# Bias tables in steps inside the first feed-forward part, and a separate operand place at the value stage

## The chip, the cores and the metric

The kernel runs on one core of one Trainium2 chip. Times are device microseconds of one execution; the time before is the median of three runs, 1962.17 us (1961.43 to 1962.37).

The core has five engines that run their own instruction queues in order: TensorE (PE in the profile; PEld is its weight load), VectorE (DVE), ScalarE (ACT), GpSimd (POOL) and SyncE (SP). DMAs are issued from SP, POOL and, at the start, ACT.

## The reference

One encoder layer over `x` of 1024 rows by 1024 columns, float32:

- `x += 1/2 * rmsnorm(swiglu(rmsnorm(x)))`, a feed-forward part with 2816 hidden columns: `(silu(h @ w_gate) * (h @ w_up)) @ w_down`
- `x += rmsnorm(w_out of the attention)`: one projection of `rmsnorm(x)` to q, k and v; 8 heads of neighbourhood attention on a 16 by 64 grid with a learned relative bias (`na_rel_bias`, 8 x 15 x 31), and 8 heads of a mixture of three dilated windows with a bucketed relative bias (`t5_rel_bias`, 8 x 32), each group normalised
- a second feed-forward part like the first

The two relative biases depend on nothing that the layer computes. They are turned into tables in device memory before the attention reads them.

## The kernel before

**Arithmetic.** Every product is float32 made of three matmuls: each operand is split into a high part (a cast on ACT) and a low part (a subtraction on DVE), and `mm3` (lines 249 to 253) adds high*high, high*low and low*high. The large products also use a seven-product scheme on 2 by 2 blocks (`PASSES`, line 31): sums of blocks are made first (S1 to S4 of the left operand, T1 to T4 of the right), and the seven results are combined on DVE.

**Stages in order.** First feed-forward part: gate and up products of 22 hidden blocks (`PairGemm`, about 97 to 500 us of the span for its main loop), then the down products (`Passes`, 500 to 682). Then the values of the attention begin (`Passes`, passes 0 and 1 of 7, 682 to 711), then the early part of the q/k products (`PairGemm.ahead`, 8 pairs, to about 760), then the values' passes 2 to 6 (to about 824), then the q/k products' main loop (`PairGemm.run`), the attention itself, the output projection and the second feed-forward part.

**`PairGemm`** (line 323). `ahead` makes the two products of the first block column for the "early" pairs, with only the left weight blocks: `fetch_left` loads them from SP, `split_left` splits them (ACT, then DVE) into tiles of the pool `wr`, and after a split the load two pairs ahead goes out. `run` makes the rest: per early pair five products of twelve matmuls each, per other pair seven. Weights of a pair are loaded two pairs ahead (`prepare(b)`, whose last step fetches `b + 2`), then turned into T1 to T4 on DVE (lines 432 to 434) and split (lines 344 and 345). A product of pair b that needs the whole pair before (`last`, line 502) is made inside the next pair's turn. At the end of each pair `c.tick()` runs one entry of the list `c.todo`, which is how side work is given turns.

**`Passes`** (line 571). `fetch` loads two raw operand blocks from SP into the pool `pw`, and splits them into the pool `pr` (lines 602 and 603). `run` makes a pass by groups of up to four operands: for each of four row tiles all matmuls of the group go into that tile's PSUM bank, then the result is taken and `c.tick()` is called. For the feed-forward part, whose two operands both come from memory (`own`), pass 0 begins with a group of two and a group of two; for the values each pass is one group of four. `vearly` (line 1360) copies each result of the values' first two passes on ACT into one of two tiles and stores it from POOL.

**Order.** PE's order is the order of the program (`ordered()`, line 1123). The orders of ACT, DVE, POOL and SP are laid out when the kernel is built, by a planner that starts from the program's order and from its own estimates of every instruction's time, except in the first microseconds, where ACT and DVE are in the program's order too. `c.behind(f, engine)` ties what `f` issues on an engine behind the last instruction that the program has given to it so far; `queued` does that for SP and POOL.

**Places.** On-chip tiles come from pools that are opened and closed in stages. A new pool reuses the space of closed ones, and a tile in it is free when the older tiles in that space have been used for the last time. At the start of the values the pools `pr` (three buffers), `pw` (two) and `vt` (two) lie in space of the feed-forward part; when pass 1 ends they close, and `wr` (three buffers of a high and a low tile) opens in the same space for the early q/k pairs.

**The bias tables.** `build_bias` (line 741) is called between the values' passes 3 and 4. It issues, all DMAs from POOL: a small load; twice a pair of loads, one matmul of the one-hot matrix (line 755), an addition on DVE (756), a store of the small table (757) and a write of 8 x 128 rows of 511 numbers (760); a memset and a write of 1536 KB of the mask value (762, 763); eight gathers of short rows into `stk` (765); and sixteen copies from `stk` into the table `nb` (768). Nothing ties the loads of `rel` to the place of the call, and the planner has put those eight DMAs into the first 40 us.

Of the kernel before, what the change touches and what calls it, by code (L numbers as in the profile page):

```python
# [23 lines left out]
NEG = -1e30  # L24
# [298 lines left out]
class PairGemm:  # L323
# [4 lines left out]
    def __init__(self, c, op, srcs, early, sink):  # L328
        self.c, self.op, self.srcs, self.early, self.sink = c, op, srcs, early, sink
        self.n, self.raw, self.w, self.kept = len(srcs), {}, {}, {}  # L330
# [42 lines left out]
    def split_left(self, b):  # L373
        if b < self.early:
            self.w[b] = self.split(self.raw.pop(b), "g")
            self.fetch_left(b + 2)
# [194 lines left out]
class Passes:  # L571
# [4 lines left out]
    def __init__(self, c, n, left, right, take, last=None):  # L576
        self.c, self.left, self.right, self.take = c, left, right, take
        self.own = not isinstance(left, Operand)
        groups = [list(range(i, min(i + 4, n))) for i in range(0, n, 4)]
        self.groups = [groups] * 6 + [last or groups]  # L580
        if self.own:
            self.groups[0] = [groups[0][:2], groups[0][2:]] + groups[1:]
        self.todo = deque((p, g[j:j + 2]) for p in range(7) for g in self.groups[p] for j in range(0, len(g), 2))
        self.ready = deque()

    def fetch(self, w=None, raws=()):
# [4 lines left out]
        if w is None:  # L591
            w = c.pr.tile([P, 1 + self.own, 2, 2, T], F32R, tag="w", name="pw")
            w = [w[:, side] for side in range(1 + self.own)]
        for side in range(1 + self.own):
            raw = raws.popleft() if raws else c.pw.tile([P, 2, T], F32, tag="raw", name="praw")
            if side < self.own:
                nc.sync.dma_start(raw[:, :m], self.left[a][ids[0]:ids[0] + m].rearrange("i p x -> p i x"))
            else:
                for j, i in enumerate(ids):
                    nc.sync.dma_start(raw[:, j], self.right(i)[b])  # L600
            hi, lo = [w[side][:, h, :m] for h in range(2)]
            nc.scalar.copy(hi, raw[:, :m])  # L602
            nc.vector.tensor_sub(lo, raw[:, :m], hi.bitcast(F32))  # L603
        for j, i in enumerate(ids):
            lhs = [w[0][:, h, j, :] for h in range(2)] if self.own else [h[:, i, :] for h in self.left.x[a]]
            self.ready.append((lhs, [w[-1][:, h, j, :] for h in range(2)]))
# [134 lines left out]
def build_bias(c, rel, t5, onehot, lncount):  # L741
# [4 lines left out]
    t5t = c.bp.tile([32, 8], F32, tag="b0", name="t5t")  # L746
    nc.gpsimd.dma_start(t5t, t5.rearrange("h b -> b h"))
    for i in range(2):
        oh = c.bp.tile([P, T], F32, tag="oh", name="oh")
        cols = slice(511 * i, 511 * i + 511)  # L750
        nc.gpsimd.dma_start(oh[:32, :511], onehot[:, cols])
        lc = c.bp.tile([P, T], F32, tag="lc", name="lc")
        nc.gpsimd.dma_start(lc[:8, :511], lncount[:, cols].broadcast_to([8, 511]))
        ps = c.pst.tile([P, 4, P], F32, tag="tr", name="tabp").rearrange("p a b -> p (a b)")
        nc.tensor.matmul(ps[:8, :511], t5t, oh[:32, :511], start=True, stop=True)
# [5 lines left out]
    neg = c.bp.tile([P, T], F32, tag="oh", name="neg")  # L761
    nc.gpsimd.memset(neg[:, :384], NEG)
    nc.gpsimd.dma_start(c.nb.rearrange("h p r e -> p h (r e)"), neg[:, :384].unsqueeze(1).broadcast_to([P, 8, 384]))
    for cc in range(8):
        nc.gpsimd.dma_start(stk[cc], rel[:, :, 7 - cc:31 - cc])
    for r in range(16):
        r0 = min(max(r - 4, 0), 8)
        nc.gpsimd.dma_start(c.nb[:, r * 8:r * 8 + 8, r0:r0 + 8, :].rearrange("h c r e -> c h (r e)"),
                            stk[:, :, r0 - r + 7:r0 - r + 15, :].rearrange("c h r e -> c h (r e)"))
# [339 lines left out]
def layer(tc, a, out):  # L1109
    nc = tc.nc  # L1110
    c = Ctx(tc)
    with ExitStack() as ctx:
# [58 lines left out]
        def one_a_turn(steps, n, first):  # L1171
            plan(n, {first + i: [f] for i, f in enumerate(steps)})
# [11 lines left out]
        def early_pools(stack, n=3):  # L1184
            c.wr, c.sp = pool("wr", 3, stack), pool("sp", n, stack)
# [7 lines left out]
        def ffn(which, op, prep, pg, get, turns, sums, more, post, pre, src, dst, begin=None):  # L1193
# [24 lines left out]
            one_a_turn(sums, NF, NF - 3 - len(sums))  # L1218
            prep2, ps = sub(), []

            def final():
# [9 lines left out]
                ps[0].fetch([w0[:, i] for i in range(2)], raws[:2])  # L1231
                ps[0].fetch([w.rearrange("p (h j) x -> p h j x", h=2) for w in w1], raws[2:])
# [62 lines left out]
        with ExitStack() as order:  # L1295
# [12 lines left out]
            def begin(pg):  # L1308
# [25 lines left out]
                for b in range(2):  # L1334
                    pg.mm(acc[b], pg.w[b], 0, A11, cols=slice(256, 512))
                    s1.append(pg.save(b, acc[b]))
                    if b:
# [12 lines left out]
                                    a["ffn1_post_g"], a["mix_pre_g"], x0, x1, begin)  # L1350
# [5 lines left out]
            c.pr, c.pw, c.vt = pool("pr", 3, e), pool("pw", 2, e), pool("vt", 2, e)  # L1356
# [23 lines left out]
            c.bp = pool("bp", 2, e)  # L1380
# [9 lines left out]
            build_bias(c, a["na_rel_bias"], a["t5_rel_bias"], a["onehot"], a["lncount"])  # L1390
# [211 lines left out]
```

## Time and profile before

| | |
|---|---|
| Median of three runs | 1962.17 us (1961.43 to 1962.37) |
| Profiled execution | 1956.22 us, of which the span from the first to the last instruction is 1954.4 us |
| Mean granted clock of TensorE | 0.986 |
| PE busy | 1867.5 us (96% of the span) |
| DVE busy | 1328.8 us (68%) |
| ACT busy | 807.7 us (41%) |
| POOL busy | 323.8 us (17%) |
| Moved by DMA | 398.63 MB, 204 GB/s on average |

How to read it: an engine's timeline row gives the start in microseconds, the length, the engine, the line of the kernel, the operation, the tile written and those read, and in brackets how long the engine stood idle before it and what ended that. Where several instructions are merged, the row has their count. A matmul's shown length overlaps the next one's. L603 is line 603; a helper's line (344, 345, 602, 603) is shared by many callers, so the tile names tell which work it is: `pw` and `praw` are operands of `Passes`, `graw`, `wraw`, `traw`, `whi` and `wlo` weights of `PairGemm`, `accp` and `mmp` PSUM banks, `vt` and `vs` the early values, `ha` and `hb` the values as they are combined, `gab`, `nb`, `stk`, `tab` and `neg` parts of the bias tables, `g`, `sg`, `sgt` the gate products.

### The profile page before, as it was taken

The numbers are of one execution on the slowest core, as the hardware profiler recorded it, in microseconds if no ns is written. First come the engines' busy times: TensorE is split into PE (matmuls) and PEld (weight loads), VectorE is DVE, ScalarE is ACT, GpSimd is POOL, SyncE is SP. The second block draws the span as 40 slices with busy tenths as digits, with TensorE's granted clock in tenths as the row PEclk, the third lists the DMA queues.
The fourth block names the chain that finished last, engine by engine and source line by source line (L and its number), as shares of the span: only waits on it lengthen the run. The fifth ranks groups of instructions, "written<-read, shape, count | busy, mean of one in ns | idle before, by whom it ended". The sixth has DMA issues, their size and how long they took to land.

```text
span 1954.4 us, 25575 instructions
## 1 busy us (share of the span) xinstructions
PE 1867.5 (96%) x9044; PEld 1557.4 (80%) x9044; DVE 1328.8 (68%) x2235; ACT 807.7 (41%) x1463; POOL 323.8 (17%) x520
## 2 busy tenths in 40 slices
PE   5999999999999999999999788998999999999997
PEld 4788888888888778778898777877888888888886
DVE  5778776765656785567576565676788777755567
ACT  4522233333534454133676555454222333345333
POOL 2101111111000123323444220021011111110000
PEclk8999999999999999999999899999999999999999
DMA  6645565546876667868998982475556665476663
GB/s 244 214 169 178 178 236 195 209 165 252 306 255 206 237 242 263 245 195 246 208 190 158 160 147 47 137 264 205 172 177 203 232 229 185 160 255 226 203 226 140
DMA packets 170433, 398.63 MB, mean 204 GB/s; under 512 B 20080, under 2 KB 41504, under 8 KB 170304
## 3 DMA queue, kind: packets, MB, share of 16 engines
q1 hardware_dynamic: 118800, 222.34, 36.2%
q0 software_dynamic: 50640, 172.55, 28.0%
q10 hardware_dynamic: 864, 2.10, 0.3%
q8 instruction: 71, 1.16, 0.3%
q14 instruction: 58, 0.48, 0.1%
HBM read 272.55 MB, written 127.26 MB: 205 GB/s over the span
## 4 chain that ended last, share of the span: by engine, by line
PE 76%; DVE 7%; DMA 7%; issue 5%; ACT 2%; POOL 2%; SPq 1%; DVEq 0%; POOLq 0%; ACTq 0%
PE mmp L253 15%; PE mmp L251 15%; PE mmp L252 14%; PE accp L251 8%; PE accp L252 8%; PE accp L253 8%; PE po L953 2%; DMA wraw<-in_wqk_dram 2%; PE ptp L859 2%; PE trp L159 1%; PE po L1053 1%; DMA st<-qk 1%; PE sp L933 1%; DMA qk<-qk 1%; DVE wlo L345 1%
## 5 line engine op out<-in xcount | busy, mean ns | idle before, releaser
L251 PE MATMUL mmp<-x,whi 128*128 128x512 f32 (+1 forms) x1464 | 581.1, 397 | 8.2 <-ACT whi L344 3.5
L253 PE MATMUL mmp<-x,wlo 128*128 128x512 f32 (+1 forms) x1464 | 576.4, 394 | 1.1 <-DVE wlo L345 1.1
L252 PE MATMUL mmp<-x,whi 128*128 128x512 f32 (+1 forms) x1464 | 575.8, 393 | 0.6 <-DVE x L161 0.5
L251 PEld LDWEIGHTS mmp<-x,whi 128*128 128x128 f32 x1464 | 278.6, 190 | 68.9 <-ACT whi L344 4.2
L253 PEld LDWEIGHTS mmp<-x,wlo 128*128 128x128 f32 x1464 | 278.5, 190 | 62.4 <-DVE wlo L345 1.9
L252 PEld LDWEIGHTS mmp<-x,whi 128*128 128x128 f32 x1464 | 278.8, 190 | 59.7 <-DVE x L161 1.5
L603 DVE TENSOR_TENSOR pw<-praw,pw 128x1024 fp32r<-128x1024 f32 (+1 forms) x182 | 199.2, 1139 | 121.8 <-ACT pw L602 121.6
L602 ACT CAST pw<-praw 128x1024 fp32r<-128x1024 f32 (+1 forms) x182 | 169.0, 982 | 205.6 <-PE accp L253 163.3
L344 ACT CAST whi<-wraw 128x1024 fp32r<-128x1024 f32 x129 | 135.2, 1050 | 249.0 <-PE mmp L252 227.4
L251 PE MATMUL accp<-pw 128*128 128x512 f32 x600 | 234.5, 391 | 0.0
L253 PE MATMUL accp<-pw 128*128 128x512 f32 x600 | 233.8, 390 | 0.0
L252 PE MATMUL accp<-pw 128*128 128x512 f32 x600 | 233.7, 390 | 0.0
L345 DVE TENSOR_TENSOR wlo<-wraw,whi 128x1024 fp32r<-128x1024 f32 x129 | 157.6, 1224 | 24.0 <-ACT whi L344 23.7
L253 PEld LDWEIGHTS accp<-pw 128*128 128x128 f32 x600 | 112.7, 188 | 23.7
L251 PEld LDWEIGHTS accp<-pw 128*128 128x128 f32 x600 | 112.7, 188 | 23.1
L252 PEld LDWEIGHTS accp<-pw 128*128 128x128 f32 x600 | 112.8, 188 | 22.9
L549 POOL DMA_DIRECT2D g<-sg x44 | 23.8, 541 | 473.3 <-DVE sg L542 286.0
L505 DVE TENSOR_TENSOR c<-mmp,u 128x512 f32<-128x512 f32 x52 | 35.9, 691 | 82.9 <-PE mmp L253 82.6
L363 ACT COPY s<-mmp 128x512 f32<-128x512 f32 x52 | 30.5, 586 | 148.8 <-PE mmp L253 147.2
L344 ACT CAST whi<-traw 128x512 fp32r<-128x512 f32 x52 | 32.3, 621 | 117.5 <-DVE traw L433 58.8
L161 DVE TENSOR_TENSOR x<-trp,x 128x512 fp32r<-128x512 f32 x84 | 57.2, 688 | 34.7 <-ACT x L160 34.7
L432 DVE TENSOR_TENSOR wraw<-wraw 128x1024 f32<-128x1024 f32 x52 | 63.6, 1224 | 23.1 <-DMA wraw<-in_wqk_dram 13.5
(229 smaller groups left out, 2781.5 us busy)
## 6 DMA issues: line engine op xcount, KB each, us to landing
praw<-g SPq DMA_DIRECT2D x70, 512.0 KB
wraw<-in_wg_dram SPq DMA_DIRECT2D x44, 512.0 KB
wraw<-in_wu_dram SPq DMA_DIRECT2D x44, 512.0 KB
tr<-in_wd_dram SPq DMA_DIRECT2D x44, 512.0 KB
g<-sg POOLq DMA_DIRECT2D x88, 256.0 KB, 3.7
ts<-tr POOLq DMA_DIRECT2D x22, 1024.0 KB, 4.7
praw<-ts SPq DMA_DIRECT2D x88, 256.0 KB
praw<-in_wd_dram SPq DMA_DIRECT2D x66, 256.0 KB
```

Source lines behind the costliest of these rows:

```text
L161: nc.vector.tensor_sub(lo, ps, hi.bitcast(F32))
L251: nc.tensor.matmul(out, ahi, bhi, start=start, stop=False, skip_group_check=go_on)
L252: nc.tensor.matmul(out, ahi, blo, start=False, stop=False, skip_group_check=go_on)
L253: nc.tensor.matmul(out, alo, bhi, start=False, stop=stop, skip_group_check=go_on)
L344: nc.scalar.copy(hi, raw)
L345: nc.vector.tensor_sub(lo, raw, hi.bitcast(F32))
L432: nc.vector.tensor_sub(r[:, 0:2], r[:, 1:3], r[:, 0:2])
L505: nc.vector.tensor_add(c21, d, u2)
L602: nc.scalar.copy(hi, raw[:, :m])
L603: nc.vector.tensor_sub(lo, raw[:, :m], hi.bitcast(F32))
L859: nc.tensor.transpose(ps[:, j, :], src[:, j * P:(j + 1) * P], c.ident)
L953: nc.tensor.matmul(po[:, un * 2 + j], pt[:, 2 * j + t, :], rhs, start=t == 0, stop=t == 1)
```

## The change

**Bias tables.** `build_bias` becomes `bias_steps`, a list of seven steps, each tied behind POOL's last instruction: load of the first one-hot half, first table, load of the second half, second table, the mask write with the eight gathers, and eight and eight of the row copies. The first feed-forward part gets them as `tables`; its main loop runs one at the end of each of the pairs 1 to 7 (turns count from 0), of 22. The pool `bp` is opened there with one buffer. The call between the values' passes 3 and 4 is gone.

**Values.** Pass 0 now always begins with two groups of two operands, for the values as well. A new pool `p0` with one buffer (a high and a low tile) is opened in space of its own; the first fetch of the values is issued before the side work of the stage is planned and is split into `p0`. The pool `pr` has two buffers in place of three. Pass 0 has eight turns, so the side work of the stage is planned over twelve turns in place of eight, with the same work at the turns that answer to the old ones, and one more entry.

**Early q/k pairs.** `PairGemm` gets a field `own`, set to `p0` for the q/k products: every third early pair (0, 3, 6) is split into `p0`, the others into `wr`, which has two buffers in place of three. Pair 0 is split at the twelfth turn of the value stage, not when `ahead` begins.

```diff
     def split_left(self, b):
         if b < self.early:
-            self.w[b] = self.split(self.raw.pop(b), "g")
+            self.w[b] = self.split(self.raw.pop(b), "g", self.own if b % 3 == 0 else None)
             self.fetch_left(b + 2)
...
-        if self.own:
-            self.groups[0] = [groups[0][:2], groups[0][2:]] + groups[1:]
+        self.groups[0] = [groups[0][:2], groups[0][2:]] + groups[1:]
...
-def build_bias(c, rel, t5, onehot, lncount):
+def bias_steps(c, rel, t5, onehot, lncount):
...
+    def load(i):
+        tt, oh, lc = got[i] = [c.bp.tile(n, F32, tag=t, name=t) for n, t in (([32, 8], "tt"), ([P, T], "oh"), ([P, T], "lc"))]
         cols = slice(511 * i, 511 * i + 511)
+        nc.gpsimd.dma_start(tt, t5.rearrange("h b -> b h"))
         nc.gpsimd.dma_start(oh[:32, :511], onehot[:, cols])
         nc.gpsimd.dma_start(lc[:8, :511], lncount[:, cols].broadcast_to([8, 511]))
+
+    def table(i):
...
+    def stack():
...
+    def rows(rs):
+        for r in rs:
...
+    steps = [lambda: load(0), lambda: table(0), lambda: load(1), lambda: table(1), stack,
+             lambda: rows(range(8)), lambda: rows(range(8, 16))]
+    return [lambda f=f: c.behind(f, POOL) for f in steps]
...
             pg.begin_rest()
-            one_a_turn(sums, NF, NF - 3 - len(sums))
+            if tables:
+                c.bp = pool("bp", 1, w)
+            one_a_turn(NF, (tables, 1), (sums, NF - 3 - len(sums)))
...
-            c.pr, c.pw, c.vt = pool("pr", 3, e), pool("pw", 2, e), pool("vt", 2, e)
+            c.pr, c.pw, c.vt = pool("pr", 2, e), pool("pw", 2, e), pool("vt", 2, e)
...
-            plan(8, {0: [lambda: fin.scale(4, 4), A(4, 5)], 4: [U(4)], 5: [lambda: queued(pg.start)]})
+            p0 = pg.own = pool("p0", 1, prep, side="right")
+            vp.fetch([[p0.tile([P, 2, T], F32R, tag="g" + h, name="pw0" + h) for h in ("hi", "lo")]])
+            plan(12, {0: [lambda: fin.scale(4, 4), A(4, 5)], 8: [U(4)], 9: [lambda: queued(pg.start)],
+                      11: [lambda: pg.split_left(0)]})
             vp.run(0, 1, upto=1)
             e.close()
-            early_pools(e, 2)
+            early_pools(e, 2, 2)
...
             pg.fetch(0)
             pg.fetch(1)
-            build_bias(c, a["na_rel_bias"], a["t5_rel_bias"], a["onehot"], a["lncount"])
             vp.run(4, 5)
```

More of the change, by code (lines that the diff above doesn't have):

```diff
@@ L592, in fetch @@
             w = c.pr.tile([P, 1 + self.own, 2, 2, T], F32R, tag="w", name="pw")
-            w = [w[:, side] for side in range(1 + self.own)]
+            w = [[w[:, side, h] for h in range(2)] for side in range(1 + self.own)]
         for side in range(1 + self.own):
@@ L600, in fetch @@
                     nc.sync.dma_start(raw[:, j], self.right(i)[b])
-            hi, lo = [w[side][:, h, :m] for h in range(2)]
+            hi, lo = [x[:, :m] for x in w[side]]
             nc.scalar.copy(hi, raw[:, :m])
@@ L604, in fetch @@
         for j, i in enumerate(ids):
-            lhs = [w[0][:, h, j, :] for h in range(2)] if self.own else [h[:, i, :] for h in self.left.x[a]]
-            self.ready.append((lhs, [w[-1][:, h, j, :] for h in range(2)]))
+            lhs = [x[:, j, :] for x in w[0]] if self.own else [h[:, i, :] for h in self.left.x[a]]
+            self.ready.append((lhs, [x[:, j, :] for x in w[-1]]))
     def run(self, *which, upto=6):
@@ L745, in build_bias @@
     tab = c.dr.tile([2, 8, T], F32, name="tab")
[L746 to L749, printed above, removed]
+    got = {}
+    def load(i):
+        tt, oh, lc = got[i] = [c.bp.tile(n, F32, tag=t, name=t) for n, t in (([32, 8], "tt"), ([P, T], "oh"), ([P, T], "lc"))]
         cols = slice(511 * i, 511 * i + 511)
+        nc.gpsimd.dma_start(tt, t5.rearrange("h b -> b h"))
         nc.gpsimd.dma_start(oh[:32, :511], onehot[:, cols])
-        lc = c.bp.tile([P, T], F32, tag="lc", name="lc")
         nc.gpsimd.dma_start(lc[:8, :511], lncount[:, cols].broadcast_to([8, 511]))
+    def table(i):
+        tt, oh, lc = got.pop(i)
         ps = c.pst.tile([P, 4, P], F32, tag="tr", name="tabp").rearrange("p a b -> p (a b)")
-        nc.tensor.matmul(ps[:8, :511], t5t, oh[:32, :511], start=True, stop=True)
+        nc.tensor.matmul(ps[:8, :511], tt, oh[:32, :511], start=True, stop=True)
         nc.vector.tensor_add(lc[:8, :511], ps[:8, :511], lc[:8, :511])
@@ L760, in build_bias @@
         nc.gpsimd.dma_start(dst, tab[i, :, :511].unsqueeze(1).broadcast_to([8, P, 511]))
[L761 to L769, printed above, removed]
+    def stack():
+        neg = c.bp.tile([P, T], F32, tag="oh", name="neg")
+        nc.gpsimd.memset(neg[:, :384], NEG)
+        nc.gpsimd.dma_start(c.nb.rearrange("h p r e -> p h (r e)"), neg[:, :384].unsqueeze(1).broadcast_to([P, 8, 384]))
+        for cc in range(8):
+            nc.gpsimd.dma_start(stk[cc], rel[:, :, 7 - cc:31 - cc])
+    def rows(rs):
+        for r in rs:
+            r0 = min(max(r - 4, 0), 8)
+            nc.gpsimd.dma_start(c.nb[:, r * 8:r * 8 + 8, r0:r0 + 8, :].rearrange("h c r e -> c h (r e)"),
+                                stk[:, :, r0 - r + 7:r0 - r + 15, :].rearrange("c h r e -> c h (r e)"))
+    steps = [lambda: load(0), lambda: table(0), lambda: load(1), lambda: table(1), stack,
+             lambda: rows(range(8)), lambda: rows(range(8, 16))]
+    return [lambda f=f: c.behind(f, POOL) for f in steps]
 class QKPairs:
@@ L1191, in gate_pairs, with ffn @@
             return PairGemm(c, op, [(wg[f], wu[f]) for f in range(NF)], early, GatePairs(c, which))
-        def ffn(which, op, prep, pg, get, turns, sums, more, post, pre, src, dst, begin=None):
+        def ffn(which, op, prep, pg, get, turns, sums, more, post, pre, src, dst, begin=None, tables=()):
             w = sub()
```

22 lines of the change are left out of this document (13 added, 9 removed).

## The prediction

> **What bounds the kernel now.** I read the page first, then busy time by stage over the stretch that the diff touches, then TensorE's (PE's) timeline there for every pause, and last the engines that end these pauses.
>
> ```profile
> span 1954.4 us, 25575 instructions
> ```
>
> The windows by stage; the first numbers after the length are PE, PEld, DVE, ACT and POOL busy, then the granted clock, the DMA share and GB/s:
>
> ```profile
> 97.00:500.00 403.00, 403.00 (x1762) 330.90 (x1761) 294.71 (x364) 132.19 (x174) 52.77 (x93) 1.00 0.57 202
> ...
> 682.00:716.00 34.00, 28.66 (x127) 21.43 (x127) 28.38 (x53) 17.37 (x29) 8.68 (x16) 1.00 0.68 243
> ...
> 786.00:804.00 18.00, 16.07 (x66) 11.53 (x65) 13.03 (x18) 4.71 (x5) 8.98 (x14) 1.00 0.74 263
> ...
> 837.00:845.00 8.00, 6.02 (x20) 4.46 (x19) 4.28 (x6) 2.74 (x4) 1.44 (x2) 0.79 0.35 98
> ```
>
> The kernel is bound by PE. In the first feed-forward part (97 to 500) PE has no gap at all (403.00 / 1762, 0.23 us a matmul), so anything added there costs at once if it stops PE, and nothing if it doesn't. In the value stage three short stretches leave PE idle: 34.00 - 28.66 = 5.34 us where the values begin, 1.93 us at 786 to 804, 1.98 us at 837 to 845. In the last one the clock is also granted at only 0.79 over 8 us, which loses (1 - 0.79) x 8 = 1.68 us more. Together 10.93 us: that is the ceiling of what the value stage can give back. The pauses one by one, PE's timeline (start, length, what, and in brackets the idle time before it and its releaser):
>
> ```profile
> 683.21 0.50 PE L251 MATMUL accp<-pw,x 128*128 128x512 f32 x1 [0.78 <-ACT pw L602]
> 684.73 0.50 PE L252 MATMUL accp<-pw,x 128*128 128x512 f32 x1 [1.02 <-DVE pw L603]
> ...
> 686.61 0.50 PE L252 MATMUL accp<-pw,x 128*128 128x512 f32 x1 [0.20 <-DVE pw L603]
> ...
> 698.77 0.50 PE L252 MATMUL accp<-pw,x 128*128 128x512 f32 x1 [0.74 <-DVE pw L603]
> ...
> 713.03 0.50 PE L251 MATMUL mmp<-x,whi 128*128 128x512 f32 x1 [1.66 <-ACT whi L344]
> 714.31 0.50 PE L253 MATMUL mmp<-x,wlo 128*128 128x512 f32 x1 [0.54 <-DVE wlo L345]
> ...
> 787.00 1.88 PE L755 MATMUL tabp<-oh,t5t 32*8 32x511 f32 x4
> ...
> 803.51 0.50 PE L252 MATMUL accp<-pw,x 128*128 128x512 f32 x1 [1.93 <-DVE pw L603]
> ...
> 839.56 0.63 PE L251 MATMUL mmp<-x,whi 128*128 128x512 f32 x1 [1.98 <-DVE c L497]
> ```
>
> **The change part by part.**
>
> (a) **A place of its own for the first values' weights.** Today the first weight split runs on ACT only when the feed-forward part's last matmul is over, though its load was issued long before:
>
> ```profile
> 659.76 27.63 SPq L600 DMA_DIRECT2D praw<-in_wv_dram  x8
> ```
>
> ```profile
> 682.12 1.03 ACT L602 CAST pw<-praw 128x1024 fp32r<-128x1024 f32 x1
> ...
> 695.92 0.59 ACT L1362 COPY vt<-accp 128x512 f32<-128x512 f32 x1 [2.08 <-DMA vs<-vt]
> 696.41 1.05 ACT L602 CAST pw<-praw 128x1024 fp32r<-128x1024 f32 x1
> ```
>
> With a place that no feed-forward operand holds, the split can run in ACT's and DVE's gaps before 682. The first pass is also cut into two groups of two operands, so PE needs only the first fetch for its first 24 matmuls (24 x 0.23 = 5.5 us, to 687.8); the second, split from 682.12 on as the first is today, is done by 684.73 as that is. So 0.78 + 1.02 + 0.20 = 2.00 us goes. Bounds 0 (the planner leaves the split where it is) and 2.00; I take 2.00, because the load goes out 22 us early and the place, beside the normalised rows' tiles, is held by no operand of the last passes.
>
> What becomes late next: the pause of 0.74 us at 698.77 stays, since the fourth fetch still needs a buffer that is read until the pass ends (696.41 follows that end). And the four results of the pass now come 6 matmuls apart (1.4 us) at its very end, not 12 plus pauses apart. They share two copy tiles, each freed by a store:
>
> ```profile
> DMA to landing us min/median/max: 2.3/4.0/6.9
> ```
>
> That is the landing of vs<-vt. The third copy on ACT must wait for the first store: copy 0.59, issue about 0.3, landing 4.0, so about 5.0 us after the first result; the pass ends 3 x 1.4 = 4.1 us after it. If ACT's order has the third copy ahead of the fourth fetch's split, as at 695.92 and 696.41 today, that split is late by 0.9 + 0.5 = 1.4 us. Queued behind the waiting copy on ACT are this split and the transposes' casts; PE waits for the split. Bounds: 0 (split first) and 4.3 (a landing of 6.9 instead of 4.0 adds 2.9). I take 1.4, by the median row.
>
> (b) **The first q/k pair's weights.** They are split only after the last value result:
>
> ```profile
> 711.93 1.05 ACT L344 CAST whi<-graw 128x1024 fp32r<-128x1024 f32 x1
> ```
>
> In the new place, free once the first value group is done, the split can run before. 1.66 + 0.54 = 2.20 us goes. The second pair still gets buffers only at the stage's end: cast 1.05 and subtraction about 1.2 behind the last copy, some 2.9 us, against 12 matmuls (2.7 us) of the first pair; 0.3 us is late next. Gain 1.9; bounds 0 and 2.2. Three rotating places (own, and two in the pool) replace three in the pool, so later pairs find a free one as before.
>
> (c) **The bias tables leave the value stage.** PE's four table matmuls take 1.88 us now and as much in the feed-forward part, where PE is full: 0 in sum. The pause at 803.51 is DVE's: its queue stood 4.97 us before a q/k weight's load, which shared the DMA engines with the tables' writes.
>
> ```profile
> 799.90 1.22 DVE L432 TENSOR_TENSOR wraw<-wraw 128x1024 f32<-128x1024 f32 x1 [4.97 <-DMA wraw<-in_wqk_dram]
> ...
> 802.24 1.22 DVE L603 TENSOR_TENSOR pw<-praw,pw 128x1024 fp32r<-128x1024 f32 x1
> ```
>
> ```profile
> 800.03 1.06 ACT L602 CAST pw<-praw 128x1024 fp32r<-128x1024 f32 x1 [0.26 <-PE accp L253]
> ```
>
> Without DVE's backlog the subtraction at 802.24 could start when the cast ends, at 801.09: 1.1 of the 1.93 us goes, the rest hangs on PE itself releasing the operand. Bounds 0 and 1.93; I take 1.1.
>
> (d) **POOL's queue.** Its rows show why the q/k stage starts badly:
>
> ```profile
> 818.95 0.56 POOL L768 DMA_DIRECT2D nb<-stk  x1 [14.80 <-DMA gab<-tab]
> 821.05 4.44 POOL L768 DMA_DIRECT2D nb<-stk  x8 [1.54 <-DMA gab<-tab]
> 825.48 1.70 POOL L1384 DMA_DIRECT2D v<-ha  x3
> 827.17 4.26 POOL L1384 DMA_DIRECT2D v<-hb  x8
> ```
>
> ```profile
> 837.61 0.69 DVE L470 TENSOR_TENSOR u<-mmp,s 128x512 f32<-128x512 f32 x1 [3.36 <-PE mmp L253]
> ...
> 838.82 0.69 DVE L497 TENSOR_TENSOR c<-mmp,v 128x512 f32<-128x512 f32 x1
> ```
>
> The value stores wait behind the tables, and the q/k stage's tiles (L497's among them) lie where the values lay. PE paused 1.98 us for L497 and then ran at the lower clock: 1.98 + 1.68 = 3.66 us. With the tables gone the stores go out as DVE writes the values, some 6 us earlier at the last row, and the planner need not put L497 behind L470. Bounds 0 (same order on DVE) and 3.66; I take 3.66, as that wait ends in this queue.
>
> Here a rule stands beside the row. The Trainium skill, "TensorE: Matmul & The Clock Gate", section "HAM oscillation — how this bites in real kernels", has the clock fall only for idle gaps beyond about 3.4 us. By it a gap of 1.98 us would have cost 1.98 alone, the sum below would be 5.8 and the time 1956.4. The row of 837 to 845 differs: 0.79 after a gap of 1.98; the measurement decides.
>
> (e) **What the tables do beside the feed-forward part.** Their bulk, from the list of DMA issues (KB each, landing):
>
> ```profile
> gab<-tab POOLq DMA_DIRECT2D x2, 2044.0 KB, 20.5
> ...
> nb<-neg POOLq DMA_DIRECT2D x1, 1536.0 KB, 8.4
> ```
>
> The two big writes overlapped; one turn apart each is about 20.5 / 2 = 10.25 us of DMA. The turns fall at the end of pairs 2 and 4. A pair here is five products of twelve matmuls, 60 x 0.23 = 13.7 us; the c of 152.90 below is pair 3's and lies after the second product of pair 4, which so ends near 161 us, and pair 2 near 134. What they can delay is the weights of a pair two ahead:
>
> ```profile
> 141.94 0.59 SPq L339 DMA_DIRECT2D wraw<-in_wu_dram  x1
> ```
>
> ```profile
> 146.66 1.22 DVE L432 TENSOR_TENSOR wraw<-wraw 128x1024 f32<-128x1024 f32 x1
> ...
> 152.90 0.69 DVE L505 TENSOR_TENSOR c<-mmp,u 128x512 f32<-128x512 f32 x1 [1.41 <-PE mmp L253]
> 153.81 1.23 DVE L345 TENSOR_TENSOR wlo<-wraw,whi 128x1024 fp32r<-128x1024 f32 x1 [0.22 <-ACT whi L344]
> ```
>
> The load lands within 146.66 - 141.94 = 4.7 us. If it is late, DVE stands at L432, and what PE needs first is the split at 153.81, done at 155.04 and read after two more products of 2.7 us behind 152.90, at 158.3: 3.3 us of cover, and DVE's idle 1.41 + 0.22 before it, 4.9 in all. If table and weights share the engines evenly, the load takes 9.4 us, 4.7 late: just covered. I take 0. Upper bound: the load waits out a whole write each time, 2 x (10.25 - 4.9) = 10.7, and 8.4 - 4.9 = 3.5 for nb, 14.2 us in all.
>
> New waits on POOL: the small table's store waits for DVE, the big write for that store. Behind them queue the gate products' stores:
>
> ```profile
> 149.98 0.54 POOL L549 DMA_DIRECT2D g<-sg  x1 [11.93 <-DVE sg L548]
> ```
>
> POOL idles 11.93 us before that row, which is the cover; uncovered, a late store holds a tile that DVE needs a pair later.
>
> (f) **The start.** Eight stk loads ran there:
>
> ```profile
> 2.33 1.14 POOL L765 DMA_DIRECT2D stk<-in_na_rel_bias_dram  x2
> ...
> 36.68 2.12 POOL L765 DMA_DIRECT2D stk<-in_na_rel_bias_dram  x4
> ```
>
> Queued behind POOL's work of the sixth turn they leave it. The two at 2.33 compete with the first activations; bounds 0 and 1.1 (their own issue time); I take 0.2.
>
> **Sum.** -2.0 + 1.4 - 1.9 - 1.1 - 3.66 - 0.2 = -7.5 us. The profiled execution took 1956.22 us (span 1954.4 and 1.82 around it), so 1948.7; the shown median of 1962.17 lies 5.95 above that execution, which gives **1954.7**.
>
> **The rivals.** *DVE's order stays*: the other three queues' order is laid out at build from estimated costs, and L497 can remain behind L470. For it: no row proves that L497 waited for a place rather than for its turn. Then (d) gives 0: -3.8, 1958.3. *ACT's copies*: (a)'s bound of 4.3 instead of 1.4, and the change's first half only moves its stall: -4.6, 1957.6. *One burst uncovered*: a single big write holds the weights 10.25 us, PE stands 5.35: -2.1, 1960.0; for it, DVE's 4.97 us before 799.90 with the same kind of traffic; against it, a pair's cover of 4.9. *The slower side, one mechanism*: every table write holds the weights for its whole length, at pairs 2 to 6, 14.2 us: +6.7, 1968.9. It decides from about 11.4 us of such stalls on. Against it: the DMA share of 0.57 in that stage.
>
> **How the numbers follow.** Forecast 0.46 (its own range 1951 to 1958), DVE's order 0.20, ACT's copies 0.05, one burst 0.16, all bursts 0.13. The best case, all upper bounds, is -10.9: 1951. The high end, 1965, leaves out most of the slower case. Changes under 0.2% (3.9 us) can't be told from none: faster is 0.46 + 0.05 + half of 0.20 = 0.61, same is the other half and the one burst, 0.26, slower 0.13.
>
> **What would show it.** No PE pause near 682 and at the start of q/k; a pause of 0.7 to 2 us remains inside the values' second pass. L497 ahead of L470 and a granted clock of 1.00 in the stretch that answers to 837 to 845. In 130 to 210 PE stays full, with L432's waits longer but under 5 us. Wrong would be: PE pauses at pairs 3 to 7 of the feed-forward part, or a pause of the old size at the q/k stage's first c.

## The result, and the profile after

The changed kernel takes 1973.46 us (median of six runs, 1971.12 to 1978.76), the kernel before beside it 1961.80 (1954.99 to 1968.95). The ratio is 1.0063, interval 1.0046 to 1.0081: 0.63% slower, 11.7 us. The forecast was 1954.7 with a range of 1951 to 1965.

The profiled execution after took 1973.99 us, with this span:

```profile
span 1972.2 us, 25575 instructions
```

The windows by stage of the changed kernel, columns as before (PE, PEld, DVE, ACT and POOL busy, granted clock, DMA share, GB/s):

```profile
97.00:500.00 403.00, 391.20 (x1680) 317.69 (x1679) 284.41 (x356) 123.86 (x163) 74.27 (x129) 0.98 0.57 200
152.00:154.00 2.00, 2.00 (x10) 1.60 (x10) 0.00 (x0) 0.00 (x0) 0.00 (x0) 1.00 0.51 208
160.00:170.00 10.00, 4.08 (x12) 3.00 (x12) 9.42 (x14) 3.13 (x4) 4.44 (x8) 0.66 0.66 187
160.66:166.58 5.92, 0.00 (x0) 0.03 (x1) 5.88 (x10) 2.95 (x4) 3.26 (x6) 0.67 0.57 166
166.58:170.00 3.42, 3.42 (x9) 2.77 (x10) 2.87 (x4) 0.00 (x0) 1.18 (x3) 0.57 0.93 260
210.00:220.00 10.00, 7.22 (x25) 5.45 (x24) 6.83 (x9) 2.61 (x3) 0.00 (x0) 0.83 0.41 147
220.00:230.00 10.00, 6.91 (x23) 5.18 (x22) 6.34 (x10) 2.20 (x3) 6.43 (x12) 0.83 0.37 116
849.00:857.00 8.00, 8.00 (x37) 6.64 (x36) 4.72 (x7) 2.62 (x4) 1.44 (x2) 1.00 0.17 43
```

PE's pauses in the same kernel, from its timeline:

```profile
166.58 0.77 PE L251 MATMUL mmp<-x,whi 128*128 128x512 f32 x1 [5.92 <-DVE v L479]
...
213.28 0.47 PE L251 MATMUL mmp<-x,whi 128*128 128x512 f32 x1 [2.78 <-DVE v L479]
...
223.76 0.50 PE L251 MATMUL mmp<-x,whi 128*128 128x512 f32 x1 [3.10 <-DVE c L498]
...
690.28 0.63 PE L159 MATMUL trp<-ident,xn 128*128 128x128 f32 x4 [1.35 <-DVE xn L200]
...
717.69 0.50 PE L251 MATMUL accp<-pw,x 128*128 128x512 f32 x1 [0.63 <-ACT pw L602]
719.43 0.51 PE L252 MATMUL accp<-pw,x 128*128 128x512 f32 x1 [1.24 <-DVE pw L603]
...
735.17 0.50 PE L253 MATMUL mmp<-x,wlo 128*128 128x512 f32 x1 [0.55 <-DVE wlo L345]
...
809.18 0.50 PE L252 MATMUL accp<-pw,x 128*128 128x512 f32 x1 [2.06 <-DVE pw L603]
```

The feed-forward stage, where PE had no gap, now has three, 5.92 + 2.78 + 3.10 = 11.8 us together, and the clock is granted at 0.66 and 0.83 in the windows around them. A lower clock costs only where PE works. Around the first pause, (1 - 0.67) x 5.92 = 2.0 us of it fall into the pause itself, and only (1 - 0.57) x 3.42 = 1.5 us into the matmuls behind it. In the two shorter pauses the clock was still 1.00 (210.50 to 213.28 and 220.60 to 223.76), and (1 - 0.83) x 10 = 1.7 us were lost behind each. That makes 11.8 us of pauses and 4.9 us of slow clock, 16.7 us. With the tables' four matmuls, which now stand here (1.9 us), and the start's 1.2 us, below under (f), the sum is 19.8 us. The changed kernel loses 20.6 us by the first combination of the last down products (first row of L659: 644.9 before, 665.5 after); the last 0.8 us are not placed.

The chain behind the first pause, from the changed kernel's timelines: the load's issue on SP, the table write's on POOL, then DVE.

```profile
144.30 0.72 SPq L339 DMA_DIRECT2D wraw<-in_wu_dram  x1
```

POOL:

```profile
142.21 1.14 POOL L763 DMA_DIRECT2D gab<-tab  x1 [2.80 <-DMA tab<-lc]
```

DVE, and below it the landing of the table write (us from issue):

```profile
157.94 1.23 DVE L433 TENSOR_TENSOR wraw<-wraw 128x1024 f32<-128x1024 f32 x1 [8.84 <-DMA wraw<-in_wu_dram]
...
165.75 0.68 DVE L479 TENSOR_TENSOR v<-mmp,u 128x512 f32<-128x512 f32 x1
```

```profile
DMA to landing us min/median/max: 16.5/17.1/17.7
```

That write of 2044 KB (`gab<-tab`) is called the spread from here on. The up weights' load was issued 2.1 us behind it and took 157.94 - 144.30 = 13.6 us where it was there within 4.7 before. DVE stood 8.84 us at L433, and everything in its queue moved back, down to L479 at 165.75. PE's next product is added into the bank that L479 reads, so PE waits for it. Beside the second spread (180.81) the load issued at 194.16 is there after 11.2 us, and the pauses at 213 and 224 us follow (DVE):

```profile
205.37 1.23 DVE L433 TENSOR_TENSOR wraw<-wraw 128x1024 f32<-128x1024 f32 x1 [6.42 <-DMA wraw<-in_wu_dram]
```

Milestones of the profiled executions (us from the start; "first scores" is PE's first matmul into `sp`), with the timed comparison of each run. The medians of the kernel before beside the later rows lie between 1959.19 and 1961.47, so rows are compared by the ratio. One of the twelve executions with the spreads in quarters took 4810.98 us and, as a slow one, is left out of that row:

| kernel | median | ratio to before, interval | first L659 | first scores | span |
|---|---|---|---|---|---|
| before | 1961.80 | | 644.9 | 937.9 | 1954.4 |
| changed | 1973.46 | 1.0063 (1.0046 to 1.0081) | 665.5 | 950.7 | 1972.2 |
| places only | 1957.71 | 0.9987 (0.9970 to 1.0003) | 645.9 | 938.2 | 1962.8 |
| tables only | 1973.53 | 1.0061 (1.0036 to 1.0087) | 663.5 | 950.5 | 1972.4 |
| spreads, rows outermost | 1970.97 | 1.0048 (1.0032 to 1.0063) | 663.4 | 949.1 | 1969.1 |
| without mask and stacking there | 1975.80 | 1.0073 (1.0050 to 1.0097) | 665.3 | 952.3 | 1975.2 |
| spreads late | 1979.27 | 1.0105 (1.0086 to 1.0125) | 650.7 | 953.7 | 1977.9 |
| spreads in quarters | 1956.12 | 0.9988 (0.9974 to 1.0002) | 650.2 | 937.0 | 1951.8 |
| all in quarters | 1956.58 | 0.9985 (0.9972 to 0.9998) | 650.4 | 935.1 | 1951.4 |
| quarters, heads outermost | 2028.84 | 1.0357 (1.0340 to 1.0374) | 724.0 | 1009.9 | 2026.3 |
| spreads in halves | 1959.12 | 0.9988 (0.9975 to 1.0000) | 651.1 | 936.2 | 1959.9 |
| quarters from turn 7 | 1957.12 | 0.9976 (0.9965 to 0.9987) | 647.3 | 934.0 | 1950.9 |
| the same, no places | 1955.93 | 0.9976 (0.9962 to 0.9990) | 648.7 | 933.7 | 1951.7 |
| whole spreads from turn 9 | 1976.01 | 1.0075 (1.0062 to 1.0088) | 668.6 | 954.8 | 1969.6 |

From the first scores to the end, code that no edit touches, these executions take between 1014.8 and 1024.6 us (span minus first scores) with no relation to the edit: 1016.5 in the kernel before, 1024.6 with the places only. So the stages are compared by the milestones, and the 5 us that the changed kernel loses after the scores are not laid to the change.

### The profile page after: what moved, and what is told of

Its sections match the earlier page's. It is cut to its first block, busy times and chain, and to the rows that moved or that the text cites. A ratio compares the mean times of both kernels' runs of the same rounds, so it can differ in the third digit from the quotient of the medians.

```text
span 1972.2 us, 25575 instructions
## 1 busy us (share of the span) xinstructions
PE 1872.5 (95%) x9044; PEld 1560.8 (79%) x9044; DVE 1328.5 (67%) x2235; ACT 808.7 (41%) x1463; POOL 325.2 (16%) x521
## 4 chain that ended last, share of the span: by engine, by line
PE 72%; DMA 11%; DVE 7%; issue 5%; ACT 3%; POOL 2%; SPq 1%; DVEq 0%; POOLq 0%; ACTq 0%
PE mmp L253 14%; PE mmp L251 14%; PE mmp L252 14%; PE accp L251 8%; PE accp L252 8%; PE accp L253 8%; DMA wraw<-in_wu_dram 2%; PE po L963 2%; PE ptp L869 1%; PE po L1063 1%; PE trp L159 1%; DMA obn<-ob 1%; DVE wlo L345 1%; DMA wraw<-in_wqk_dram 1%; DMA qk<-qk 1%
## 5 line engine op out<-in xcount | busy, mean ns | idle before, releaser
L345 DVE TENSOR_TENSOR wlo<-wraw,whi 128x1024 fp32r<-128x1024 f32 x129 | 157.7, 1224 | 27.6 <-ACT whi L344 27.5
L433 DVE TENSOR_TENSOR wraw<-wraw 128x1024 f32<-128x1024 f32 x52 | 63.6, 1224 | 35.0 <-DMA wraw<-in_wu_dram 23.4
```

What stands on the lines that cost most here:

```text
L345: nc.vector.tensor_sub(lo, raw, hi.bitcast(F32))
L433: nc.vector.tensor_sub(r[:, 0:2], r[:, 1:3], r[:, 0:2])
```

## The experiments

**Which half.** The tables go back between value passes 3 and 4, the places stay:

```diff
-                                    a["ffn1_post_g"], a["mix_pre_g"], x0, x1, begin,
-                                    bias_steps(c, a["na_rel_bias"], a["t5_rel_bias"], a["onehot"], a["lncount"]))
+                                    a["ffn1_post_g"], a["mix_pre_g"], x0, x1, begin)
...
             pg.fetch(1)
+            build_bias(c, a["na_rel_bias"], a["t5_rel_bias"], a["onehot"], a["lncount"])
             vp.run(4, 5)
```

> The changed kernel with the bias tables built where they were before, between value passes 3 and 4; the places of its own (first values' weights, every third early q/k pair) stay. Theory: the whole loss comes from the tables beside the first feed-forward part (two pauses of about 9.3 us in the 150 to 230 us of the profile), and the places give back what the milestones show: 2.5 us before the first values and up to 4 us by the first q/k pair. Then this kernel stands at 1955 to 1960 us against 1962 for the kernel before, and its feed-forward stage shows no pause at 166 and 223 us. Rival: the places themselves disturb the first feed-forward part or the start (the order of the pools and the planner); then it stays at 1965 us or more, and the pauses stay.

Measured 1957.71 us, within the theory's range; by the interval it can't be told from no change. Its feed-forward stage has no pause:

```profile
97.00:500.00 403.00, 403.00 (x1762) 330.68 (x1761) 294.64 (x364) 132.27 (x173) 52.67 (x93) 1.00 0.57 201
```

The other half alone, an edit of the kernel before:

```diff
-            one_a_turn(sums, NF, NF - 3 - len(sums))
+            if tables:
+                c.bp = pool("bp", 1, w)
+            one_a_turn(NF, (tables, 1), (sums, NF - 3 - len(sums)))
...
-            build_bias(c, a["na_rel_bias"], a["t5_rel_bias"], a["onehot"], a["lncount"])
             vp.run(4, 5)
```

> The kernel before with only the tables moved beside the first feed-forward part; no place of its own for anything. Theory: the two pauses are there with the same causes (a raw load that lands 13 us after its issue beside the first table's spread, and an 11 us one beside the second), 18.6 us, less what leaves the value stage (about 3 to 4 us): 1974 to 1979 us. Rival: the gain of the value stage came all from the tables' leaving and none from the places; then about 1972, no slower than the whole change.

Measured 1973.53 us, between the two expectations and equal to the whole change. It reaches L659 18.6 us later than the kernel before. So the tables are the loss, and the places neither cause it nor gain anything measurable beside it.

**What of the tables.** The mask write, the gathers and the stacked rows are given out after value pass 3, as before; only the two tables stay in the feed-forward part:

```diff
-    return [lambda f=f: c.behind(f, POOL) for f in steps]
+    c.late = steps[4:]
+    return [lambda f=f: c.behind(f, POOL) for f in steps[:4]]
...
             pg.fetch(1)
+            for f in c.late:
+                f()
```

> The changed kernel with only the loading, making and spreading of the two tables beside the first feed-forward part; the fill with -1e9-like values and the stacking of the other bias are given out where they were before, after value pass 3. Theory: the second pause (2.8 + 3.1 us and the clock after them, some 9 us) comes from the stacking's gathers and the fill, which run together with the end of the second spread; without them it goes and the first pause stays: 1963 to 1966 us. Rival: the second spread alone delays the raw load issued at 194 us; then the second pause stays, and the time with it, 1971 to 1975 us.

My theory fell: 1975.80 us, 0.8 above the rival's range, and the second pair of pauses is still there, as these rows of its PE show:

```profile
166.58 0.76 PE L251 MATMUL mmp<-x,whi 128*128 128x512 f32 x1 [5.73 <-DVE v L479]
...
212.47 0.47 PE L251 MATMUL mmp<-x,whi 128*128 128x512 f32 x1 [1.81 <-DVE v L479]
...
222.69 0.80 PE L251 MATMUL mmp<-x,whi 128*128 128x512 f32 x1 [4.45 <-DVE c L498]
```

The opposite: all stays but the two spreads.

```diff
         nc.gpsimd.dma_start(tab[i, :, :511], lc[:8, :511])
+
+    def write(i):
         g = c.gab[i]
...
+    c.write_gab = lambda: c.behind(lambda: [write(i) for i in range(2)], POOL)
...
             pg.fetch(1)
+            c.write_gab()
             vp.run(4, 5)
```

> The changed kernel; of the tables' steps only the two spreads (2 MB each, 8 heads by 128 rows) are given out at the old place, after value pass 3; loading, the small matmuls, the fill and the stacking stay beside the first feed-forward part. Theory (the spreads alone cause both pauses): the pause at 166 us goes, and the second pair of pauses too; the first feed-forward part is as before, and the value stage has its old pauses: 1956 to 1962 us. Rival (the fill of 1.5 MB with the gathers does as much as a spread): one pause of some 9 us stays, near 195 to 225 us, 1965 to 1970 us.

The pauses at 166 and 213 to 224 us are gone (first L659 at 650.7 in place of 665.5), with the mask write and the gathers still there: the two spreads cause them. (Two new ones of 1.47 and 0.53 us, at 289 and 310 us, were not traced.) The total missed the expectation: 1979.27 us. Tied to that place the two spreads met the loads of the q/k weights, as this kernel's POOL, DVE and PE show:

```profile
773.85 2.19 POOL L765 DMA_DIRECT2D gab<-tab  x2 [0.62 <-issue]
```

DVE:

```profile
797.68 1.23 DVE L433 TENSOR_TENSOR wraw<-wraw 128x1024 f32<-128x1024 f32 x1 [15.42 <-DMA wraw<-in_wqk_dram]
```

PE:

```profile
799.65 0.77 PE L251 MATMUL accp<-pw,x 128*128 128x512 f32 x1 [9.23 <-DVE hb L653]
```

These loads went out from SP at 778.78 to 780.69, 5 to 7 us behind the spreads. In the kernel before the spreads went out later than the loads that PE needed next:

```profile
798.65 2.16 POOL L760 DMA_DIRECT2D gab<-tab  x2 [0.49 <-DMA tab<-lc]
```

**Why a spread holds a load: engines or bytes.** First the order of the write's dimensions, nothing else:

```diff
-        dst = bass.AP(tensor=g.tensor, offset=g.offset, ap=[[P * 640, 8], [641, P], [1, 511]])
-        nc.gpsimd.dma_start(dst, tab[i, :, :511].unsqueeze(1).broadcast_to([8, P, 511]))
+        dst = bass.AP(tensor=g.tensor, offset=g.offset, ap=[[641, P], [P * 640, 8], [1, 511]])
+        nc.gpsimd.dma_start(dst, tab[i, :, :511].unsqueeze(0).broadcast_to([P, 8, 511]))
```

> The changed kernel, with the spread of each table written with its 128 rows outermost in place of its 8 heads: same elements, same place in the queue. Theory A (the spread runs on 8 of the 16 DMA engines, because its outermost size is 8, and the weights' load waits for those 8): the spread now uses all 16 engines, lands in about 10 us in place of 17, the raw load beside it lands in about 5 to 10 us, the first pause of 5.9 us shrinks to under 1 and its slow clock with it: 1963 to 1966 us. Theory B (the bytes and small rows of the spread alone, in whatever order): the mean share of the engines stays at 0.5 for 17 us or goes to 1.0 and the load waits as long; no change, 1971 to 1975 us, or later.

Measured 1970.97 us, outside A's range and at the lower edge of B's. Theory A was right on the spread and wrong on the load. With rows outermost the mean share of the DMA engines beside the first spread rises (windows of 146 to 156 us; the changed kernel first, then this one):

```profile
146.00:156.00 10.00, 10.00 (x46) 8.18 (x45) 1.92 (x2) 1.05 (x1) 0.00 (x0) 1.00 0.68 249
```

```profile
146.00:156.00 10.00, 10.00 (x46) 8.18 (x45) 1.92 (x2) 1.05 (x1) 0.00 (x0) 1.00 0.92 267
```

and it lands in 12.9 us in place of 17.1 (landing of `gab<-tab` in this kernel):

```profile
DMA to landing us min/median/max: 12.9/12.9/13.0
```

But the load still waits until about then, and the pause with it; both tables now make the same one (DVE of this kernel):

```profile
156.96 1.23 DVE L433 TENSOR_TENSOR wraw<-wraw 128x1024 f32<-128x1024 f32 x1 [8.28 <-DMA wraw<-in_wu_dram]
...
192.71 1.23 DVE L433 TENSOR_TENSOR wraw<-wraw 128x1024 f32<-128x1024 f32 x1 [8.35 <-DMA wraw<-in_wu_dram]
```

Then the size of one write: four pieces of two heads, 511 KB each, rows outermost, one a turn.

```diff
+    def piece(i, h):
         g = c.gab[i]
...
+        dst = bass.AP(tensor=g.tensor, offset=g.offset + h * P * 640, ap=[[641, P], [P * 640, 2], [1, 511]])
+        nc.gpsimd.dma_start(dst, tab[i, h:h + 2, :511].unsqueeze(0).broadcast_to([P, 2, 511]))
...
-    steps = [lambda: load(0), lambda: table(0), lambda: load(1), lambda: table(1), stack,
+    pieces = [[lambda i=i, h=h: piece(i, h) for h in range(0, 8, 2)] for i in range(2)]
+    steps = [lambda: load(0), lambda: table(0), *pieces[0], lambda: load(1), lambda: table(1), *pieces[1], stack,
```

> The changed kernel with each spread given out in four pieces of two heads (0.5 MB), rows outermost, one piece in each turn, so that the tables' steps fill turns 1 to 15 in place of 1 to 7; the fill and the gathers stay one burst. Theory (a weights' load that meets a spread lands when the whole burst has landed, whatever engines it takes, so only the size of a burst counts): each load lands 2 to 4 us later than undisturbed, inside the cover of 4.9 us, no pause at 166 us and none at the second table; the time falls to 1954 to 1960 us, if the fill's burst makes no pause. Rival (the number of small packets counts, not the size of one burst): the same 18 us are lost in smaller parts over eight turns, 1970 to 1975 us.

Beside it the same pieces with the heads outermost:

```diff
-ap=[[641, P], [P * 640, 2], [1, 511]])
+ap=[[P * 640, 2], [641, P], [1, 511]])
...
-unsqueeze(0).broadcast_to([P, 2, 511])
+unsqueeze(1).broadcast_to([2, P, 511])
```

> As the kernel with the spreads in pieces of two heads, one piece a turn, but with the two heads outermost in place of the 128 rows: same bytes, same turns. Theory A (the outermost size sets how many engines write: two): a piece lands only after about 10 us (0.5 MB at a quarter of the 208 GB/s that the spread had with 8), the mean share of the engines stays near 0.1 to 0.2, and the part of a weights' load that goes over these two engines waits as long as before: pauses come back, up to 3 to 5 us in each of eight turns with the slow clock behind them, 1970 to 2000 us. Theory B (only bytes count): same time as with rows outermost, 1954 to 1960 us.

Same bytes, same turns; only the outermost dimension differs (128 rows, or two heads). Measured 1956.12 and 2028.84 us: A's way, though far beyond its sizes (2000 us at most, a landing of about 10 us). The landings of `gab<-tab` with rows outermost:

```profile
DMA to landing us min/median/max: 4.9/5.7/7.0
```

and with heads outermost:

```profile
DMA to landing us min/median/max: 15.0/16.7/18.9
```

With two heads outermost the first pieces hold a load like a whole spread (DVE):

```profile
171.51 1.23 DVE L433 TENSOR_TENSOR wraw<-wraw 128x1024 f32<-128x1024 f32 x1 [7.82 <-DMA wraw<-in_wu_dram]
...
191.60 1.23 DVE L433 TENSOR_TENSOR wraw<-wraw 128x1024 f32<-128x1024 f32 x1 [11.20 <-DMA wraw<-in_wu_dram]
```

Both loads had been issued 12.9 us earlier (SP, 158.60 and 178.69). Not all of this kernel's loss is of that kind: of the 54.5 us that PE pauses up to 510 us, 28.9 lie from 362 us on. The first pause there stands behind a POOL store that waits 30.00 us (356.05), as in the last experiment below; the others were not traced. With rows outermost the worst waits of this kind are 2.13 and 2.67 us:

```profile
178.18 1.23 DVE L433 TENSOR_TENSOR wraw<-wraw 128x1024 f32<-128x1024 f32 x1 [2.13 <-DMA wraw<-in_wu_dram]
...
193.13 1.23 DVE L433 TENSOR_TENSOR wraw<-wraw 128x1024 f32<-128x1024 f32 x1 [2.67 <-DMA wraw<-in_wu_dram]
```

The Trainium skill, "DMA: Bandwidth & Descriptors", section "Rules for kernel authors", has the outermost size below 16 confine a DMA to that many engines at most. The landings of 12.9 against 17.1 us and of 5.7 against 16.7 us agree with it.

The quarters with rows outermost came out in the range (1956.12). They leave one pause of 1.51 us at 216 us in the main loop, and the clock stays at 1.00 around it:

```profile
210.00:226.00 16.00, 14.49 (x61) 10.73 (x60) 14.41 (x21) 3.86 (x6) 6.84 (x12) 1.00 0.62 203
```

Halves for the size between:

```diff
-ap=[[641, P], [P * 640, 2], [1, 511]])
+ap=[[641, P], [P * 640, 4], [1, 511]])
...
-for h in range(0, 8, 2)]
+for h in range(0, 8, 4)]
```

> As the kernel with the spreads in pieces of two heads, first step in turn 1, but in pieces of four heads (1 MB, rows outermost). Theory (the load waits for what is left of one burst, 12 us for 2 MB, some 7 to 8 us for 0.5 MB in landings): each load that meets a piece lands about 4 to 6 us late against a cover of 4.9 us: one or two short pauses of 1 to 3 us with 3.4 us of slow clock each, 1958 to 1967 us. Rival (only whole tables hurt, or the count of packets): 1956 us as in quarters, or 1971 us as in one burst.

Measured 1959.12 us, in the range; a half lands in 8.4 us, and the three pauses it leaves in the main loop are 0.16 to 0.69 us, shorter than expected. So 1971 is out. The ratio to the kernel before is 0.9988 as for the quarters, so the two can't be told apart, and that rival stays open: halves disturb half as many turns. And the mask write and the stacking cut as well:

```diff
-    def stack():
+    def stack(h):
...
+             *[lambda h=h: stack(h) for h in range(0, 8, 2)], *[lambda r=r: rows(range(r, r + 4)) for r in range(0, 16, 4)]]
```

> As the kernel with the spreads in pieces of two heads, and the 1.5 MB fill, the eight gathers and the sixteen stacked rows are cut in four as well, one part a turn (turns 1 to 20). Theory: no burst is over 0.5 MB, no pause in the first feed-forward part: 1953 to 1958 us; if the fill's burst costs nothing, the same as the kernel with whole fill. Rival: the longer row of steps runs beside the sums' loads of turns 8 to 18 and these turn late: 1960 us or more.

Measured 1956.58 us, as with the mask write whole: that write costs nothing here that could be measured.

**When.** The pieces from turn 7 on:

```diff
-            one_a_turn(NF, (tables, 1), (sums, NF - 3 - len(sums)))
+            one_a_turn(NF, (tables, 7), (sums, NF - 3 - len(sums)))
```

> As the kernel with the spreads in pieces of two heads (1956.6 us), but the tables' first step is in turn 7 in place of turn 1 (steps in turns 7 to 21). Theory: up to the ninth pair the loads of two pairs stand 13.7 us apart, after it 19.3 us (rows of the load's issues), so a load that lands 2 to 4 us late has 5.6 us more cover there; the one pause left (1.5 us at 216 us with 3.4 us of slow clock) goes, 4.9 us: 1950 to 1953 us. Rival: the steps now lie beside the sums of turns 8 to 18 and their stores and loads on the same queues; a new pause comes there and the time stays at 1955 to 1962 us.

The same steps and the same turn 7 put into the kernel before, whose `pr`, `wr` and first group stay as they were:

> The kernel before, with the tables in pieces of two heads from turn 7 on, and no place of its own for the first values' weights or the early q/k pairs. Theory: the places are worth what they were worth with the tables at the old place (0.7 us by the first scores' milestone, 1961.5 to 1957.7 us by the medians): 1951 to 1956 us, 1 to 3 us above the kernel with both. Rival: with the tables gone from the value stage the places give nothing, or cost their copies: the same or up to 2 us below.

Measured 1957.12 and 1955.93 us, both 0.24% faster than the kernel before, the intervals clear of 1. The stage is full again (with the places; 97 to 500 us):

```profile
97.00:500.00 403.00, 403.00 (x1756) 328.89 (x1755) 293.27 (x362) 130.92 (x172) 77.25 (x134) 1.00 0.63 214
```

The median of the first missed the expected 1950 to 1953: L659 came 2.9 us earlier than with pieces from turn 1, not 4.9. The 3.4 us of slow clock that I had counted behind the pause of 1.51 us were never there (a clock of 1.00 at 210 to 226 us with the pieces from turn 1). The time lies in the rival's range, but the rival's new pause did not come. The places gave nothing, as the second rival had it.

Whole spreads as in the change, only later:

```diff
-            one_a_turn(NF, (tables, 1), (sums, NF - 3 - len(sums)))
+            one_a_turn(NF, (tables, 9), (sums, NF - 3 - len(sums)))
```

> The changed kernel with whole spreads (2 MB each, heads outermost), but the tables' steps in turns 9 to 15 in place of 1 to 7. Theory: what counts is the load's lateness (8 to 9 us past its undisturbed landing) against its cover, which is 5.6 us more where turns are 19.3 us long (4.9 + 5.6 = 10.5 us): no pause, 1951 to 1957 us. Rival: the lateness comes out longer there, or the cover is no longer than before; the pauses move with the spreads, 1965 to 1975 us.

Measured 1976.01 us, 1 us above the rival's range and not by its mechanism. The two spreads (260.82 and 303.26, landing 18.0 us) cost no pause: PE has none before 363 us. There DVE reads at 290.07 the load that SP issued at 266.89, 23 us of room for a landing of 18. What stopped PE is an order, in this kernel's timelines of SP,

```profile
289.98 0.70 SPq L308 DMA_DIRECT2D tr<-in_wd_dram  x1
...
343.87 0.55 SPq L307 DMA_DIRECT2D tr<-in_wd_dram  x1
```

POOL,

```profile
357.05 0.79 POOL L319 DMA_DIRECT2D ts<-tr  x1 [31.70 <-DVE tr L318]
357.83 0.55 POOL L562 DMA_DIRECT2D g<-c  x1
```

DVE,

```profile
362.65 0.69 DVE L498 TENSOR_TENSOR c<-mmp,v 128x512 f32<-128x512 f32 x1 [5.89 <-DMA g<-c]
```

and PE:

```profile
363.39 0.79 PE L251 MATMUL mmp<-x,whi 128*128 128x512 f32 x1 [6.47 <-DVE c L498]
```

SP's order, laid out when the kernel is built, has two turns without a down-weight load; POOL's store of that sum waits 31.70 us, and the gate product's store of c behind it holds the tile that DVE needs. Four more pauses of 1.09 to 2.54 us follow up to 453 us and were not traced; why the planner chose that order was not tried either.

## Why the prediction was wrong

**Step (e) failed**, the 0 us for the tables beside the feed-forward part. It measured 16.7 us of pauses and slow clock; its upper bound was 14.2. The rival "every table write holds the weights for its whole length" (0.13, 1968.9) comes nearest to what happened, at the place and by the mechanism it named, though by the two spreads alone: the mask write, 3.5 of its 14.2 us, cost nothing that could be measured, and each spread cost more than its share. Four parts of step (e) were wrong:

- *"If table and weights share the engines evenly, the load takes 9.4 us."* It took 13.6. The load did not get an even share; it landed about when the spread had. Why is not shown.
- *10.25 us for one spread*, half of the two overlapping ones. Alone it takes 17.1 us. The DMA share was 0.51 where it ran alone (152 to 154 us) and 1.01 where the two overlapped in the kernel before:

```profile
806.00:816.00 10.00, 10.00 (x46) 8.29 (x45) 3.36 (x5) 1.05 (x1) 0.00 (x0) 1.00 1.01 230
```

  With the faster write that has its rows outermost, this shows why halving was wrong: one spread runs on part of the engines, and two beside each other used more of them. The outermost 8 stood in line 759 of the code.
- *4.9 us of cover.* I followed the split at L345. The row with the least slack was v, which reads the bank that PE needs again at 158.3. It stood in the queue at

```profile
156.28 0.69 DVE L478 TENSOR_TENSOR v<-mmp,u 128x512 f32<-128x512 f32 x1
```

  in the kernel before and was done at 156.97: 1.3 us of slack and DVE's idle 1.41 + 0.22 before it. An 8.84 us wait became a 5.92 us pause: 2.9 us of cover.
- *The clock.* 4.9 of the 16.7 us are the lower clock after the pauses. I had priced that in (d), from a row, and left it out of the bound in (e).

The argument against the rival, a DMA share of 0.57, was an average over 403 us. It is 0.57 in the changed kernel's row too.

**(a) and (b)** gave the sum they said, and it did not last. -2.0 + 1.4 - 1.9 = -2.5; from L659 to the first copy of a q/k result on ACT (L807) the kernel before takes 80.1 us, the changed one 77.6. The pauses are not the ones expected, so the agreement is in part luck: 1.35 us at a transpose is new, 0.63 + 1.24 us came inside the pass. And the kernel pair that differs in the places alone with the feed-forward stage undisturbed (quarters from turn 7) shows the gain handed back: to that copy 78.1 us with places and 81.1 without, from there to the first scores 208.5 and 203.9. With the places the next pass meets this, on PE,

```profile
791.87 0.61 PE L252 MATMUL accp<-pw,x 128*128 128x512 f32 x1 [2.08 <-DVE pw L603]
```

on DVE,

```profile
782.43 1.23 DVE L433 TENSOR_TENSOR wraw<-wraw 128x1024 f32<-128x1024 f32 x1 [3.15 <-DMA wraw<-in_wqk_dram]
```

and on ACT:

```profile
783.69 1.06 ACT L344 CAST whi<-wraw 128x1024 fp32r<-128x1024 f32 x1 [6.04 <-DVE wraw L433]
...
788.19 1.99 ACT L602 CAST pw<-praw 128x1024 fp32r<-128x1024 f32 x2
```

The loads for the main loop's first pair are issued at the same time in both (SP, 777.30 and 776.90), though the stage with the places is further on. DVE and ACT stand for them, and the values' split stands behind them. With a pause of 0.49 us just before it the 2.08 us also brought the clock down, to 0.83 over 10 us:

```profile
788.00:798.00 10.00, 7.44 (x25) 5.45 (x24) 7.89 (x10) 2.18 (x3) 0.56 (x1) 0.83 0.59 195
```

0.49 + 2.08 + 1.7 = 4.3 us, nearly all of the 4.6 us handed back. Without the places PE is full from 743 to 850. That SP's order alone keeps the loads there is argued, not tried.

**(c)** fell: -1.1 was taken; the pause is 2.06 us after and 1.93 before. It is the wait just shown.

**(d)** held: L498 stands ahead of L471, PE runs through, and the clock is 1.00 in 849 to 857; -3.66. The kernel with only the spreads back in the value stage has the 1.98 us pause again, and the kernel with the mask write and the stacking back there has not, so it is the spreads' leaving that does it. From the first q/k copy to the first k row the changed kernel gained 6.0 us, 1.9 of them the moved matmuls; (c) and (d) had -4.76, measured -4.1.

**(f)** -0.2 came out at about +1.2 by the first v of the main loop (100.9 before, 102.1 after). The kernel that leaves these loads at the start shows +1.0 at L659 as well; the gathers are not the cause. Over the profiled executions of all these kernels that first v lies between 100.9 and 102.7 us, so the +1.2 may be no more than a difference between executions; it stays open.

Without (e) the sum of -7.5 would still have been 3 to 5 us too good: the kernels with places and the spreads in quarters stand 3.1 (from turn 1) and 4.1 us (from turn 7) under the kernel before. The rivals *DVE's order* and *ACT's copies* did not come: (d) held, and ACT's copies show no 4.3 us stall.

## What to carry to other kernels

A write moved into a full stage is to be priced by the latest load that meets it: how many DMA engines its outermost dimension gives it, how long it lands alone, and the row of the waiting queue with the least slack, not the first one that a reader finds. The average share over the stage did not show that. Cutting the write into small pieces over many turns, rows outermost, from turn 7 on, turned 12 us of loss into 4 us of gain; and time gained in one stage should be followed to the next load that does not come earlier.

## What was not expected of the hardware

- A write of 2044 KB landed in 17.1 us with 8 outermost and in 12.9 with 128; 511 KB in 5.7 us with 128 and in 16.7 with 2. The quarter on two is as slow as the whole on eight.
- A 512 KB load that met such a write was there 13.6 us after its issue (2044 KB, 8 outermost), 13.1 (2044 KB, 128), 12.9 (511 KB, 2) and 6.9 to 7.8 (511 KB, 128). In the kernel before, the same load was there within 4.7, and those that DVE waited for after 5.8 to 6.1. In these runs the neighbour's own landing set it more than its bytes.
- With pauses of 2.78 and 3.10 us the granted clock was 0.83 over the 10 us window of each, with one of 5.92 us 0.66, and there the clock fell before the pause was over. Near 2 us it went both ways: 0.79 over 8 us with 1.98 us in the kernel before, but 1.00 over 10 us with 1.93 us there (800 to 810) and with 2.06 us in the changed kernel (806 to 816). The Trainium skill, "TensorE: Matmul & The Clock Gate", section "HAM oscillation — how this bites in real kernels", names gaps beyond about 3.4 us; the 1.98, 2.78 and 3.10 us here don't agree.
